# A hybrid attention and recurrence block on one core: the rank of a pair's operations, and which projections stand beside the first and the last pair

## The chip, the cores and the metric

The kernel runs on one core of a Trainium2 chip. The metric is device time in microseconds (us) of one execution, the median of several runs. A core has TensorE (PE; its weight loads are PEld), VectorE (DVE), ScalarE (ACT), GpSimd (POOL) and SyncE (SP). Each works through its own queue in order. DMA transfers are issued here by SP and POOL.

## The reference

One transformer-like block on 256 tokens of width 2048, with a context of 256 tokens that serves attention and the start state of the recurrence. All in float32:

```python
mod = silu(c) @ w_ada + b_ada;  shift, scale, gate = split(mod, 3)
xn = rmsnorm(x) * (1 + scale) + shift        # the same for the context: cn
aq, ak, av, ag, hq, hff, hfb, hi, hg, ma, mb = split(xn @ w_in)    # w_in: 2048 x 19456
att = window_attention(rope(aq), rope(ak), av, k_ctx, v_ctx, sink) * silu(ag)
f = lb + (1 - lb) * sigmoid(z)               # z: hff forward, hfb backward; 16 heads of 128
s_f, s_b = final states of the context's recurrences
o = forward scan + backward scan of S <- f * S + (1 - f) v^T, read with silu(hq)
hg_branch = rmsnorm(o, per head) * silu(hg)
y = sigmoid(ma + b0) * (hg_branch @ w_o_hgrn) + sigmoid(mb + b1) * (att @ w_o_attn)
out = rmsnorm(x + gate * (y @ w_out))
```

## The kernel before, in words

**A projection in chunks.** TensorE multiplies float32 as high and low parts in the type fp32r. A chunk of weights is 512 KB: SP loads it into one of four `raw` buffers (L66), ScalarE copies the high part into `wh` (L76), VectorE subtracts to get the low part `wl` (L77), three buffers each, and TensorE runs matmuls high by high, low by high and high by low (L91, L92 and L94 where tokens are stationary, L145 and L148 where weights are). The generators `proj_tok_g` (8 chunks) and `proj_col_x_g` (4 chunks) yield after each chunk, so that chunks can be placed between other work. Their sums lie in two of four PSUM banks `pj`.

**Order.** A scheduler orders each engine's instructions ahead of time, by a simulated time line: among those that could run it takes the one that ranks highest. Rank is program order, raised by `tc.high_priority(...)`; a chunk's two splits are raised by `PRIO` (L75), a pair's operations are not raised. In blocks with `manual_schedule` TensorE keeps the program's order; instructions outside of such a block can be placed into its gaps.

**Stages.** First norms, modulation and the first forget gates. Then the input stage (to about 655 us): values, keys and forget gates, with `quad_tok` and `quad_col` (a Strassen-like form of the product, seven products per block, L592 to L670). Each of the 13 calls of `quad_col` writes forget gates `F` (a tile of tag `F0`, two buffers) to DRAM, and then takes a step of `gate` (L670): the last third of the modulation, the vector `gate` of the reference, is computed on VectorE, 32 chunks of `w_ada` at two instructions each (L201 to L203). In the input stage its weights go through POOL's queue into an `F0` buffer too (`wg`, L193), later through SP's into `raw`.

**Pairs.** Then the 16 heads of the recurrence in eight pairs, from L1157. `load_forgets` brings the gates of both directions back (tags `F0`, and `F1` with one buffer) and `ctx_decay` scans the context's part on VectorE (L776 to L781). `pair` is a generator of small operations: the context's decays are turned on TensorE (L921), products grow over levels 1 to 64 on VectorE (`grow`, L899 to L905) with copies on ScalarE (`copies`, L831 and L834), blocks of decay-weighted scores come from matmuls of 32 rows (`level`, L858), then the state at the middle (`own`, L979, and L984 on VectorE), the output (`ob`, L996 to L998), the norm (L1004, L181, L182, L1008) and, as `turned`, the transposition into `bH` and `bL` (L1016 to L1022), which the output projection reads; `turned` runs early in the next pair.

A pair yields how many steps of TensorE work shall follow (1.5, 0.5, 1.5, 3, 1 and 1, together 8.5 steps of two chunks), and `weave` puts chunks of other projections there: `inputs` takes 13 items of `side_work` (output gates, merge gates, attention gates; nine items each, of which eight are chunks) and the next pair's query projection (4 chunks). For the last pair it takes 17 items and what is left of the side work. `with_gates` adds a step of `gate` after every six chunks. The first query projection (L1162) stands directly ahead of the first pair.

**After the pairs.** `part_a` (L1180) multiplies the recurrence's branch by `w_o_hgrn` in four blocks of 512 columns, eight chunks each; the chunk at row 256 k needs heads 2 k and 2 k + 1. A step of `gate` is taken ahead of every second chunk. Then attention, the second output projection and the final one with its norm.

Of the kernel before, what the change touches and what calls it, by code (L numbers as in the profile page):

```python
# [14 lines left out]
P = 128  # L15
# [6 lines left out]
PRIO = 100000  # L22
# [16 lines left out]
def block_kernel(ctx: ExitStack, tc: tile.TileContext, x, c, cx, c_ctx, w_ada, b_ada, norm_gain, w_in,  # L39
# [29 lines left out]
    def wchunk(w, row0, nk, col0, ncol):  # L69
        cl = col0 if isinstance(col0, tuple) else (col0,)  # L70
        raw, rv = wload(w, row0, nk, cl, ncol)
        h = wp.tile([P, 1024], F32R, tag="wh", name="wh", bufs=3)
        lo = wp.tile([P, 1024], F32R, tag="wl", name="wl", bufs=3)
        n = len(cl) * nk * ncol
        with tc.high_priority(PRIO):  # L75
            act.activation(h[:, :n], raw[:, :n], AF.Copy)  # L76
            dve.tensor_tensor(lo[:, :n], raw[:, :n], h[:, :n].bitcast(F32), op=ALU.subtract)  # L77
        parts = [(h[:, g * nk * ncol: (g + 1) * nk * ncol].rearrange("p (k c) -> p k c", k=nk),
                  lo[:, g * nk * ncol: (g + 1) * nk * ncol].rearrange("p (k c) -> p k c", k=nk)) for g in range(len(cl))]
        return parts if isinstance(col0, tuple) else parts[0]  # L80
# [6 lines left out]
    def mm_high_first(parts):  # L87


        for o, s, m, first, _ in parts:  # L90
            pe.matmul(o, s[0], m[0], start=first, stop=False)  # L91
            pe.matmul(o, s[1], m[0], start=False, stop=False)  # L92
        for o, s, m, _, last in parts:
            pe.matmul(o, s[0], m[1], start=False, stop=last)  # L94

    def bank(name="pj"):
        return pj.tile([P, 512], F32, tag="pj", name=name)

    def proj_tok_g(w, col0, src, toks):


        banks = [bank() for _ in toks]
        for k0 in range(0, KT, 2):
            h, lo = wchunk(w, k0 * P, 2, col0, 512)
            mm_high_first([(banks[i], src(k0 + j, t), (h[:, j, :], lo[:, j, :]), k0 + j == 0, k0 + j == KT - 1)
                           for j in range(2) for i, t in enumerate(toks)])
            yield len(toks) * 6 * 512
        return banks
# [126 lines left out]
    with pl("st", reuse_waits="tile") as st:  # L235
# [201 lines left out]
        def take(g, n):  # L437
            for _ in range(n):
                next(g, None)
# [71 lines left out]
    def pairs_of(a):  # L511
        return a.rearrange("p (a t) -> p a t", a=2)

    def run(g):
        for _ in g:
            pass
# [26 lines left out]
    gate = gates()  # L543

    with pl("sp", reuse_waits="tile") as sp:
# [74 lines left out]
        def quad_col(d, h0):  # L620

            co = (C_FF, C_FB)[d] + h0 * HD
            b = {n: wload(w_in, 1024 * (n[0] == "2"), 8, (co + HD * (n[1] == "2"),), HD)[0]
                 for n in ("11", "12", "22", "21")}
            m_ = [bank8() for _ in range(3)]
            into = {0: (0, True), 1: (1, True), 2: (0, False), 3: (1, False), 4: (0, False), 5: (2, True), 6: (0, False)}
            sg = [base.tile([P, 512], F32, tag="sm", name="sg", bufs=3) for _ in range(2)]
            s15 = fp.tile([P, 2, 512], F32, tag="F1", name="s15")
            su = None

            def joined(m, s, dst):


                dve.tensor_tensor(s, m, s, op=ALU.add)
                dve.tensor_tensor(dst, pairs_of(s[:, :T]), pairs_of(s[:, T:]), op=ALU.add)

            for (i, _, mv), src in zip(ORDER, combos(b)):
                h, lo = [a.rearrange("p (k c) -> p k c", k=8) for a in two(src)]
                z, fresh = into[i]
                for k in range(8):  # L640
                    pe.matmul(m_[z].rearrange("p (z a t) -> p z a t", z=2, a=2), h[:, k, :], mv(k),  # L641
                              start=fresh and k == 0, stop=False, skip_group_check=True)
                for k in range(8):
                    pe.matmul(pairs_of(m_[z][:, :T]), lo[:, k, :], mv(k)[:, 0], start=False, stop=k == 7,  # L644
                              skip_group_check=True)
                with tc.high_priority(2 * PRIO):
                    if i < 2:
                        act.activation(s15[:, i, :], m_[i], AF.Copy)
                    elif i == 2:
                        su = base.tile([P, 512], F32, tag="bb", name="su", bufs=2)  # L650
                        act.activation(su, m_[0], AF.Copy)
                    elif i == 3:
                        joined(m_[1], su, half(sg[1], 0))
                    elif i == 4:
                        u3 = base.tile([P, 512], F32, tag="bb", name="u3", bufs=2)
                        act.activation(u3, m_[0], AF.Copy)
                        joined(u3, s15[:, 1, :], half(sg[1], 1))
                    elif i == 5:
                        joined(m_[2], s15[:, 0, :], half(sg[0], 0))
                    else:  # L660
                        act.activation(half(sg[0], 1), pairs_of(m_[0][:, T:]), AF.Copy)
                        dve.tensor_tensor(half(sg[0], 1), pairs_of(m_[0][:, :T]), half(sg[0], 1), op=ALU.add)
            F = fp.tile([P, 2, 512], F32, tag="F0", name="F0", bufs=2)
            for i in (1, 0):
                act.activation(sg[i], sg[i], AF.Sigmoid)
                act.activation(F[:, i, :], sg[i], AF.Identity, scale=lbc[:, 2 + d, h0 + i: h0 + i + 1],
                               bias=lbc[:, d, h0 + i: h0 + i + 1])
            nc.gpsimd.dma_start(F_dr[d][h0 // 2], F.rearrange("p i t -> p (i t)"))
            wg_at[:] = ["F0", 2]
            take(gate, 1)  # L670

        def quad_tok(col0, dst):

# [87 lines left out]
    bH = hp.tile([P, KT, T], F32R, name="bH")  # L761
    bL = hp.tile([P, KT, T], F32R, name="bL")
# [267 lines left out]
    def weave(g, filler):  # L1030

        ahead = 0
        for want in g:
            ahead -= want * STEP
            while ahead < 0:
                got = next(filler, None)
                if got is None:
                    break
                ahead += got
        run(filler)  # L1040
# [53 lines left out]
    def attn_gates(j):  # L1094
        for hf in range(2):
            bg = yield from proj_col_x_g(w_in, C_G + 512 * j + 256 * hf)
            for i, b in enumerate(bg):
# [4 lines left out]
                c0 = (2 * hf + i) * T  # L1102
                nc.gpsimd.dma_start(cg_dr[j][:, c0: c0 + T], sg)

    def load_forgets(n):
        F = [fp.tile([P, 2, 512], F32, tag=f"F{d}", name=f"F{d}", bufs=2 - d) for d in range(2)]
        for d in (1, 0):
            nc.gpsimd.dma_start(F[d].rearrange("p i t -> p (i t)"), F_dr[d][n])
        ctx_decay(F)
        return F  # L1110
# [5 lines left out]
            yield 0  # L1116

    side = side_work()
    SIDE = (13, 13, 13, 13, 13, 13, 13, 17)

    def inputs(n, res):

        units, F = 0, None
        for _ in range(SIDE[n]):
            got = next(side, None)
            if got is None:
                break
            units += got
            if F is None and n < 7 and units >= 4 * STEP:
                F = load_forgets(n + 1)  # L1130
            yield got
        if n < 7:
            F = F or load_forgets(n + 1)
            res[:] = [F, (yield from proj_col_x_g(w_in, C_HQ + 2 * (n + 1) * HD))]
        else:
            run(side)

    def with_gates(filler):

# [17 lines left out]
    with tc.manual_schedule(engines={mybir.EngineType.PE}):  # L1157
        wg_at[:] = []
        count = [0]
        grps = [[None] * 3 for _ in range(4)]  # L1160
        res = [load_forgets(0), None]
        res[1] = result(proj_col_x_g(w_in, C_HQ))  # L1162
        for n in range(8):
            if n % 2 == 0:
                load_values(n // 2, grps[n // 2])
                load_gate(n // 2, grps[n // 2])
            nxt = [None] * 2
            weave(pair(n // 2, n % 2, grps[n // 2], *res), with_gates(inputs(n, nxt)))
            res = nxt
            if n == 0:  # L1170
                attn_values()
        for f in done:
            f()

    def b_st(kt, t):
        sl = slice(t * P, (t + 1) * P)
        return bH[:, kt, sl], bL[:, kt, sl]


    def part_a(n):  # L1180
        by = proj_tok_g(w_oh, n * 512, b_st, range(2))
        for z in range(4):
            take(gate, 1)
            for _ in range(2):
                next(by)
        by = result(by)
        for t in range(2):
            dve.tensor_tensor(y[n][:, t, :], by[t], y[n][:, t, :], op=ALU.mult)
# [5 lines left out]
    for n in range(4):  # L1194
        part_a(n)
# [337 lines left out]
```

## Time and profile before

| | us |
|---|---|
| median of 3 runs | 1642.47 |
| lowest, highest run | 1642.16, 1650.26 |
| profiled execution, its own time | 1636.88 |
| its span, first to last instruction | 1635.1 |
| TensorE busy | 1578.3 |
| VectorE, ScalarE busy | 1190.2, 870.4 |
| mean granted TensorE clock | 0.992 |

The profile is of one execution. A row of a group gives line, engine, operation, tiles written and read, shapes, count, then busy time in us and the mean of one in ns, then the idle time of the engine ahead of them and what ended it. A row of the timeline gives start, duration, engine, line, tiles, shapes and count, and in brackets the idle time ahead and its releaser. The granted clock is a share of full speed. Tile names are those of the program, without buffer numbers.

### The profile page before, as it was taken

How to read it: one execution, taken by the hardware profiler on the slowest of the kernel's cores; microseconds unless marked ns; L12 is line 12 of the kernel's file. 1: busy time of each engine (PE TensorE's matmuls, PEld its weight loads, DVE VectorE, ACT ScalarE, POOL GpSimd, SP SyncE). 2: the span in 40 equal slices, each digit the busy share in tenths (PEclk: the TensorE clock that was granted, in tenths of full speed). 3: DMA queues.
4: the chain of work that ended last, by engine and by line, in shares of the span. 5: the costliest groups of instructions: out<-in, count | busy, mean ns of one | idle time of the engine just before them, and what ended most of it. 6: DMA issues, size and time to landing. Idle time of an engine off the chain costs nothing.

```text
span 1635.1 us, 27367 instructions
## 1 busy us (share of the span) xinstructions
PE 1578.3 (97%) x10810; PEld 1345.8 (82%) x10810; DVE 1190.2 (73%) x1745; ACT 870.4 (53%) x1356; POOL 105.8 (6%) x216
## 2 busy tenths in 40 slices
PE   7999999999999999799999999999999999899998
PEld 4667899999888888678878878788888878788887
DVE  4449677777888888678787878876656778656764
ACT  4334433434566666466665666666344666754442
POOL 2000000000000000111101110111000000000000
PEclk9999999999999999899999999999999999999999
DMA  9994533344455554766667667666665543367662
GB/s 370 386 365 155 167 130 129 131 132 136 132 174 169 165 163 156 255 225 200 229 213 248 207 204 239 207 213 229 201 190 181 160 129 103 118 235 233 219 196 88
DMA packets 234177, 318.06 MB, mean 195 GB/s; under 512 B 10400, under 2 KB 154176, under 8 KB 233280
## 3 DMA queue, kind: packets, MB, share of 16 engines
q1 hardware_dynamic: 217360, 260.03, 48.9%
q0 software_dynamic: 15968, 55.17, 9.6%
q8 instruction: 85, 1.39, 0.3%
q10 hardware_dynamic: 720, 1.11, 0.2%
q14 instruction: 44, 0.36, 0.1%
HBM read 292.67 MB, written 23.60 MB: 193 GB/s over the span
## 4 chain that ended last, share of the span: by engine, by line
PE 78%; DVE 8%; DMA 6%; ACT 4%; issue 4%; POOL 0%; DVEq 0%; POOLq 0%; ACTq 0%
PE pj L91 11%; PE pj L92 11%; PE pj L94 11%; PE pj L145 5%; PE pm L641 4%; PE pj L641 4%; PE pj L722 2%; PE pj L719 2%; PE pj L717 2%; PE pm L644 2%; PE pj L644 2%; DVE wl L77 2%; PE pj L148 2%; PE pa L319 2%; PE pm L722 2%
## 5 line engine op out<-in xcount | busy, mean ns | idle before, releaser
L77 DVE TENSOR_TENSOR wl<-raw,wh 128x1024 fp32r<-128x1024 f32 x292 | 354.7, 1221 | 170.9 <-ACT wh L76 165.8
L76 ACT ACTIVATE wh<-raw 128x1024 fp32r<-128x1024 f32 x292 | 307.3, 1060 | 275.8 <-PE pj L92 194.5
L91 PE MATMUL pj<-wh,xHL 128*128 128x512 f32 (+1 forms) x704 | 275.9, 394 | 1.2 <-ACT sg L218 0.7
L92 PE MATMUL pj<-wh,xHL 128*128 128x512 f32 (+1 forms) x704 | 270.3, 386 | 0.0
L94 PE MATMUL pj<-wl,xHL 128*128 128x512 f32 (+1 forms) x704 | 183.4, 385 | 0.4 <-DVE wl L77 0.4
L91 PEld LDWEIGHTS pj<-wh,xHL 128*128 128x128 f32 x704 | 132.8, 189 | 28.1 <-ACT sg L218 1.9
L92 PEld LDWEIGHTS pj<-wh,xHL 128*128 128x128 f32 x704 | 132.8, 189 | 24.6
L94 PEld LDWEIGHTS pj<-wl,xHL 128*128 128x128 f32 x704 | 130.1, 188 | 27.3 <-DVE wl L77 0.8
L616 ACT ACTIVATE wh<-raw 128x1024 fp32r<-128x1024 f32 x92 | 97.3, 1058 | 91.1 <-PE pj L719 28.2
L145 PE MATMUL pj<-xHL,wh 128*128 128x512 f32 x512 | 135.0, 406 | 1.6 <-ACT F L831 1.6
L616 ACT ACTIVATE wh<-T 128x1024 fp32r<-128x1024 f32 x69 | 73.2, 1060 | 110.0 <-DVE T L597 40.0
L617 DVE TENSOR_TENSOR wl<-raw,wh 128x1024 fp32r<-128x1024 f32 x92 | 111.8, 1220 | 21.9 <-ACT wh L616 21.7
L145 PEld LDWEIGHTS pj<-xHL,wh 128*128 128x128 f32 x512 | 94.9, 194 | 20.0 <-ACT F L831 1.8
L617 DVE TENSOR_TENSOR wl<-T,wh 128x1024 fp32r<-128x1024 f32 x69 | 84.2, 1221 | 24.6 <-ACT wh L616 24.1
L92 PE MATMUL pj<-wh,bL 128*128 128x512 f32 x256 | 99.5, 391 | 0.0
L91 PE MATMUL pj<-wh,bH 128*128 128x512 f32 x256 | 99.4, 390 | 0.0
L148 PEld LDWEIGHTS pj<-xHL,wl 128*128 128x128 f32 x512 | 70.4, 191 | 5.4
L148 PE MATMUL pj<-xHL,wl 128*128 128x256 f32 x512 | 71.6, 283 | 0.0
L94 PE MATMUL pj<-wl,bH 128*128 128x512 f32 x256 | 70.1, 391 | 0.0
L904 DVE TENSOR_TENSOR A<-A,X 128x512 f32<-128x512 f32 x96 | 61.9, 686 | 2.4 <-ACT Kmt L834 1.3
L597 DVE TENSOR_TENSOR T<-raw,T 128x1024 f32<-128x1024 f32 x46 | 56.2, 1221 | 0.5
L91 PEld LDWEIGHTS pj<-wh,bH 128*128 128x128 f32 x256 | 48.1, 188 | 10.0
(368 smaller groups left out, 3055.5 us busy)
## 6 DMA issues: line engine op xcount, KB each, us to landing
raw<-in_w_in_dram SPq DMA_DIRECT2D x300, 512.0 KB, 3.9
raw<-in_w_ada_dram SPq DMA_DIRECT2D x83, 512.0 KB, 7.7
raw<-in_w_o_hgrn_dram SPq DMA_DIRECT2D x32, 512.0 KB, 4.0
raw<-in_w_o_attn_dram SPq DMA_DIRECT2D x32, 512.0 KB, 4.2
F<-F POOLq DMA_DIRECT2D x29, 512.0 KB, 4.6
raw<-in_w_out_dram SPq DMA_DIRECT2D x28, 512.0 KB, 3.6
wg<-in_w_ada_dram POOLq DMA_DIRECT2D x13, 512.0 KB, 6.2
v<-vo POOLq DMA_DIRECT2D x8, 512.0 KB, 3.1
```

The costliest lines, as they stand in the source:

```text
L76: act.activation(h[:, :n], raw[:, :n], AF.Copy)
L77: dve.tensor_tensor(lo[:, :n], raw[:, :n], h[:, :n].bitcast(F32), op=ALU.subtract)
L91: pe.matmul(o, s[0], m[0], start=first, stop=False)
L92: pe.matmul(o, s[1], m[0], start=False, stop=False)
L94: pe.matmul(o, s[0], m[1], start=False, stop=last)
L145: pe.matmul(o.rearrange("p (a t) -> p a t", a=2), h[:, j, cs_], xHL[:, :, k0 + j, :T], start=k0 + j == 0, stop=False)
L148: pe.matmul(o[:, :T], lo[:, j, cs_], xH[:, k0 + j, :T], start=False, stop=k0 + j == KT - 1)
L616: act.activation(h, src, AF.Copy)
L617: dve.tensor_tensor(lo, src, h.bitcast(F32), op=ALU.subtract)
L641: pe.matmul(m_[z].rearrange("p (z a t) -> p z a t", z=2, a=2), h[:, k, :], mv(k), start=fresh and k == 0, stop=False, skip_group_check=True)
L644: pe.matmul(pairs_of(m_[z][:, :T]), lo[:, k, :], mv(k)[:, 0], start=False, stop=k == 7, skip_group_check=True)
L722: pe.matmul(o, st_(4 * s + k)[:, 0, z, :], lo[:, k, :], start=False, stop=s == 1 and k == 3 and z == 1, skip_group_check=True)
```

## The change

Four things change:

1. In `weave` each step of `pair` is made under `high_priority(2 * PRIO)`, and so is the first `load_forgets`: a pair's operations rank above the chunks' splits.
2. The first output gate (9 items of side work, 8 chunks) is computed ahead of the first query projection.
3. The last pair takes the remaining 8 items of the side work and then 7 of the 8 chunks of the first block of `part_a`, whose eighth chunk stays behind the pair.
4. The last four calls of `quad_col` (h0 of 12 and 14) take no step of `gate`.

```diff
@@ quad_col
-            take(gate, 1)
+            if h0 < 12:
+                take(gate, 1)
@@ weave
-        for want in g:
+        while True:
+            with tc.high_priority(2 * PRIO):
+                want = next(g, None)
+            if want is None:
+                break
             ahead -= want * STEP
@@
+    first_a = proj_tok_g(w_oh, 0, b_st, range(2))
@@
-    SIDE = (13, 13, 13, 13, 13, 13, 13, 17)
+    SIDE = (13, 13, 13, 13, 13, 13, 13, 8)
@@ inputs, the last pair
-            run(side)
+            yield from side
+            for _ in range(7):
+                yield next(first_a)
@@ ahead of the pairs
-        res = [load_forgets(0), None]
+        with tc.high_priority(2 * PRIO):
+            res = [load_forgets(0), None]
+        take(side, 9)
         res[1] = result(proj_col_x_g(w_in, C_HQ))
@@ part_a
-        by = proj_tok_g(w_oh, n * 512, b_st, range(2))
-        for z in range(4):
+        by = first_a if n == 0 else proj_tok_g(w_oh, n * 512, b_st, range(2))
+        for z in range(1 if n == 0 else 4):
             take(gate, 1)
-            for _ in range(2):
-                next(by)
+            take(by, 1 if n == 0 else 2)
```

`take(g, n)` advances a generator n times; `b_st`, which hands out `bH` and `bL`, is only moved up.

More of the change, by code (lines that the diff above doesn't have):

```diff
@@ L1103, in attn_gates, with b_st @@
                 nc.gpsimd.dma_start(cg_dr[j][:, c0: c0 + T], sg)
+    def b_st(kt, t):
+        sl = slice(t * P, (t + 1) * P)
+        return bH[:, kt, sl], bL[:, kt, sl]
+    first_a = proj_tok_g(w_oh, 0, b_st, range(2))
     def load_forgets(n):
@@ L1173, in block_kernel @@
             f()
-    def b_st(kt, t):
-        sl = slice(t * P, (t + 1) * P)
-        return bH[:, kt, sl], bL[:, kt, sl]
     def part_a(n):
-        by = proj_tok_g(w_oh, n * 512, b_st, range(2))
-        for z in range(4):
+        by = first_a if n == 0 else proj_tok_g(w_oh, n * 512, b_st, range(2))
+        for z in range(1 if n == 0 else 4):
             take(gate, 1)
-            for _ in range(2):
-                next(by)
+            take(by, 1 if n == 0 else 2)
         by = result(by)
```

## The prediction

> **What bounds the kernel now.** I read the page first, then the busy time by stage, then what TensorE waited for.
>
> ```profile
> PE 1578.3 (97%) x10810; PEld 1345.8 (82%) x10810; DVE 1190.2 (73%) x1745; ACT 870.4 (53%) x1356; POOL 105.8 (6%) x216
> ```
> ```profile
> 140.00:655.00 515.00, 514.16 (x3390) 472.76 (x3389) 419.24 (x443) 258.16 (x308) 26.37 (x46) 1.00 0.47 148
> 655.00:692.00 37.00, 26.71 (x135) 22.95 (x134) 25.20 (x36) 18.09 (x27) 4.67 (x16) 0.86 0.70 255
> 692.00:1128.00 436.00, 417.52 (x4156) 356.81 (x4155) 346.40 (x584) 275.16 (x527) 50.31 (x106) 0.99 0.67 219
> 1128.00:1235.00 107.00, 107.00 (x496) 88.85 (x495) 60.76 (x73) 44.82 (x56) 5.07 (x9) 1.00 0.64 201
> ```
>
> The columns are the stretch, its length, busy PE, PEld, DVE, ACT and POOL, the granted clock, the DMA share and GB/s. TensorE is the bound, and its work does not change, so the change can only win back idle time and slow clock. The input stage (140 to 655) and the first output projection (1128 to 1235) have none to give. The seam at 655 to 692 lacks 10.3 us, the pairs (692 to 1128) lack 18.5 us. The waits of TensorE name them, the seam's first (whole run), then the pair stage's:
>
> ```profile
> PE tw L921 <- DVE F L781: 10.3, 1, 10.3
> ```
> ```profile
> PE ob L998 <- DVE X L984: 10.5, 6, 3.0
> PE al L858 <- ACT so L834: 3.6, 2, 1.8
> PE pj L145 <- ACT F L831: 1.6, 1, 1.6
> PE kt L964 <- DVE A L904: 1.5, 7, 0.4
> ```
>
> Idle time also costs clock afterwards. Short stretches behind three stalls:
>
> ```profile
> 679.40:683.00 3.60, 3.60 (x13) 3.23 (x14) 3.47 (x7) 1.92 (x4) 0.00 (x0) 0.53 0.13 27
> 848.30:852.00 3.70, 3.70 (x31) 3.61 (x32) 2.04 (x5) 1.22 (x9) 0.00 (x0) 1.00 0.46 161
> 951.60:956.00 4.40, 4.14 (x43) 3.22 (x44) 4.23 (x8) 2.44 (x5) 0.00 (x0) 0.61 0.78 256
> 1057.60:1062.00 4.40, 4.35 (x14) 3.37 (x15) 4.40 (x7) 2.53 (x4) 1.08 (x2) 0.61 0.69 204
> ```
>
> Behind the 10.3 us stall the clock stands at 0.53 for 3.6 us, a loss of 3.6 x 0.47 = 1.7 us. Behind two of the short stalls it is 0.61 for 4.4 us: 2 x 4.4 x 0.39 = 3.4 us. So the seam costs 10.3 + 1.7 = 12.0 us, the pairs 18.5 + 3.4 = 21.9 us, and 33.9 us is the most that the change can win.
>
> [...]
>
> **The seam: an output gate ahead of the first pair, and no gate chunk in the last four column products.** What pair 0 waited for stands in the timeline (start, duration, engine, line, idle before):
>
> ```profile
> 643.88 0.56 POOL L668 DMA_DIRECT2D F<-F  x1 [14.62 <-ACT F L666]
> 656.36 0.71 POOL L194 DMA_DIRECT2D wg<-in_w_ada_dram  x1
> 657.65 0.55 POOL L1108 DMA_DIRECT2D F<-F  x1 [0.38 <-DVE sg L635]
> 669.83 0.53 POOL L1108 DMA_DIRECT2D F<-F  x1 [6.21 <-DVE acc L203]
> ```
> ```profile
> 667.99 1.54 DVE L203 SCALAR_TENSOR_TENSOR acc<-wg,cg,acc 128x512 f32<-128x512 f32 x2 [3.00 <-DMA wg<-in_w_ada_dram]
> 668.00 1.11 PE L148 MATMUL pj<-xHL,wl 128*128 128x256 f32 x8
> 678.61 0.68 DVE L781 SCALAR_TENSOR_TENSOR F<-F,e 128x512 f32<-128x512 f32 x1
> 679.40 1.94 PE L921 MATMUL tw<-cs,F 128*128 128x128 f32 x8 [10.29 <-DVE F L781]
> ```
>
> The last gate chunk (wg) takes one of the two F0 buffers at 656.36, lands at 668 and is used up at 669.5. Only then may pair 0's forward forgets load into that buffer, and their scans and L781 end at 679.3. TensorE ran dry at 669.1.
>
> ```profile
> F<-F POOLq DMA_DIRECT2D x29, 512.0 KB, 4.6
> ```
>
> Two edits meet here. Without the gate chunk, the F0 buffer whose content was stored at 643.88 is free at about 648.5 (4.6 us for such a store), so that load moves forward by some 15 us or more; F1 still loads at 657.65, behind L635. And eight chunks of the output gate now stand between the column products and the query projection. One chunk is 2.73 us of TensorE, by the start of the same group in two successive chunks:
>
> ```profile
> 1130.43 1.08 PE L94 MATMUL pj<-wl,bH 128*128 128x512 f32 x4
> 1133.16 1.07 PE L94 MATMUL pj<-wl,bH 128*128 128x512 f32 x4
> ```
>
> Eight are 21.8 us: TensorE has work to 669.1 + 21.8 = 690.9, and needs L781 then, not at 669. Even if nothing came earlier, 679.3 would be 11.6 us in time. So the 12.0 us goes, and the clock behind it.
>
> What is late next is weights. The loads of raw issued between 652 and 672, and the two splits that free a buffer:
>
> ```profile
> DMA to landing us min/median/max: 6.4/9.3/10.2
> ```
> ```profile
> L77 DVE TENSOR_TENSOR wl<-raw,wh 128x1024 fp32r<-128x1024 f32 x292 | 354.7, 1221 | 170.9 <-ACT wh L76 165.8
> L76 ACT ACTIVATE wh<-raw 128x1024 fp32r<-128x1024 f32 x292 | 307.3, 1060 | 275.8 <-PE pj L92 194.5
> ```
>
> With four buffers a chunk can come every (9.3 + 1.06 + 1.22) / 4 = 2.9 us, at 10.2 us every 3.1, against 2.73: over eight chunks 1.4 to 3 us, and nothing where the gate chunk that is gone makes the loads quicker. Bounds 0 and 3 us; I take 1, since the buffers start full. The gain is 11 us, with 9 and 12 as ends.
>
> **The gate chunks moved.** The pair loop has 20 gate steps before (124 half-step chunks, one in six) and 20 after (123). Four leave the column products, so three chunks and the closing sum end up in the first output projection, with three loads on SP's queue instead of POOL's.
>
> ```profile
> L203 DVE SCALAR_TENSOR_TENSOR acc<-raw,cg,acc 128x512 f32<-128x512 f32 x34 | 25.5, 749 | 25.4 <-DMA raw<-in_w_ada_dram 25.2
> L904 DVE TENSOR_TENSOR A<-A,X 128x512 f32<-128x512 f32 x96 | 61.9, 686 | 2.4 <-ACT Kmt L834 1.3 <-ACT F L831 0.5
> L905 DVE TENSOR_TENSOR X<-X 128x256 f32<-128x256 f32 (+5 forms) x48 | 11.7, 243 | 1.3
> ```
>
> Three chunks are 6 x 0.749 = 4.5 us of VectorE in a stage where it is busy 60.8 of 107 us and TensorE all of it: nothing. If one of these loads were late, the ring of raw buffers behind it would stop for a chunk, 2.7 us; that is the cost without cover.
>
> **Pairs above chunks.** One wait in its order (third pair):
>
> ```profile
> 843.72 1.06 PE L979 MATMUL al<-v,Kmt 128*128 128x128 f32 x8
> 844.39 2.36 DVE L77 TENSOR_TENSOR wl<-raw,wh 128x1024 fp32r<-128x1024 f32 x2 [3.85 <-ACT wh L76]
> 846.67 0.75 DVE L156 TENSOR_TENSOR hsum<-pj,hsum 128x256 f32<-128x256 f32 x2
> 847.34 1.11 DVE L984 SCALAR_TENSOR_TENSOR X<-so,X,al 128x128 f32<-128x128 f32 x4
> 848.25 0.49 PE L998 MATMUL ob<-X,A 128*128 128x128 f32 x2 [3.02 <-DVE X L984]
> ```
>
> L984 could start when the own state is there (844.8), but two weight splits and a sum of the next pair's queries stand ahead of it. With the pair on top it comes first, save for a split already running (up to 1.2 us). A pair asks for 8.5 steps, 17 chunks, and gets 16 or 15. Where it has 16, a chunk of 2.7 us lies between the own state and L998, and the wait goes. Where it has 15 (pairs 2, 4 and 6), three L984 of the four must pass while TensorE has 0.45 us of L996 and L997: 0.85 - 0.45 = 0.4, with part of a split about 1.0 each. So 10.5 becomes 3.
>
> The al, pj and kt waits (3.6 + 1.6 + 1.5, and small ones to 18.5 in all) come out of the chain of L904 and copies under 6 chunks (16.4 us) of cover; each of its nine links can meet a split. Not being queued behind two of them, but still behind one that runs, I take half: 8.0 becomes 4. The clock loss 3.4 becomes 1, as fewer stalls cause it. Together 21.9 becomes 8: 14 us.
>
> On the other side the splits are served later. In those 6 chunks VectorE owes the pair 12 x 0.686 + 6 x 0.243 = 9.7 us and the chunks 6 x 1.221 = 7.3: 17.0 in 16.4 us and the matmuls of the levels. The lag is under a microsecond by this, and two finished chunks (5.5 us) cover it. What it costs without the cover is the fourth rival's price. Bounds 0 and 14 us (all given back); I take 4, nearer the lag that the rows give. Net 10 us.
>
> **The last pair.** It had 15 chunks and gets 7 + 7 = 14; the output projection's first seven need only heads 0 to 13. Before, this work was taken there anyway: the matmuls on bH at 1130 and 1133 above lie ahead of the pair's own end, in
>
> ```profile
> 1136.76 0.39 PE L998 MATMUL ob<-so,A 128*128 128x128 f32 x2
> ...
> 1140.61 1.12 DVE L1008 SCALAR_TENSOR_TENSOR so<-ob,ss,gate 128x128 f32<-128x128 f32 x4
> ...
> 1146.26 0.48 ACT L1021 ACTIVATE bH<-to,cols 128x256 fp32r<-128x256 f32 x1 [1.43 <-PE to L1016]
> ```
>
> and TensorE was idle nowhere from 1128 on. So this edit has nothing to win, and it uses up the cover: from the last L998 to the end of L1008 are 4.6 us, and transposes, L1021 and its rest add about 1.7 (0.44 + 2 x 0.48 and the hand-over): 6.3 us before heads 14 and 15 are there. The eighth chunk waits for them and holds one of three wh buffers, so only two chunks of the next block, 5.5 us, can be pulled ahead. That leaves 0.8; the own state with one chunk of cover less, and L984 right before L998, add some 1.7. I take a loss of 2.5 us, between 0 and 6.3.
>
> **Sum.** -11 - 10 + 2.5 = -18.5 us on the profiled execution of 1636.9 us (span 1635.1): 1618.4. The median of the three runs, 1642.47, is 5.6 us above that execution, and I apply the difference to it: 1624.
>
> **Rivals.** First, the order on VectorE gives back all that it wins (pair waits go, splits come late by as much): only seam and tail count, 1642.5 - 11 + 2.5 = 1634. For it: VectorE is busy 346 of 436 us, and 17.0 of 16.4 us in the long step. Against: the waits named are mostly one short instruction behind two long ones.
>
> Second, the seam only changes its wait: loads of eight more chunks don't keep up in a stretch of 255 GB/s, and half of the 12 us returns as waits for raw: 1624 + 5 = 1629. Against: among the waits of TensorE in the pair stage, at 219 GB/s, stands no load.
>
> Third, all goes: 33.9 us, less nothing at the tail: 1609.
>
> Fourth, slower. The order is fixed ahead, and VectorE takes its instructions in that order; a pair's L904 put ahead of a split waits there for its copies on ScalarE, and the split behind it waits too.
>
> ```profile
> L834 ACT ACTIVATE Kmt<-A 128x512 f32<-128x512 f32 x30 | 20.7, 715 | 15.1 <-DVE A L904 14.5 <-DVE A L899 0.6
> ```
>
> A round has two copies, 1.43 us; four rounds are 5.7 us of VectorE standing still in the long step, against one finished chunk of 2.7: 3.0 us a pair, 24 us over eight, none of the old waits gone: 1642.5 - 11 + 2.5 + 24 = 1658. It decides from 16.7 / 8 = 2.1 us a pair on. For it: L203 already stood 25.2 us at VectorE's head, waiting for its load. Against: L904 itself stood for copies only 1.8 us in 96. [...]
>
> **How the numbers follow.** My forecast 0.50 (1617 to 1631); first rival 0.17, second 0.12, third 0.12, fourth 0.09. Half a per cent, 8.2 us, is about what a measurement of this kernel can tell from no change: faster means below 1634.3. The first rival lies on that line and gives half to "same"; with a little of the second: faster 0.80, same 0.11, slower 0.09. The range to leave out two in ten takes in most of the first three rivals: 1612 to 1638.
>
> **What would show it.** Right: no wait at tw L921 in the seam, and clock 1.00 there; L984 directly behind L979 on VectorE, ob waits near 3 us; the last gate chunks behind 1128 instead of ahead of it; TensorE short of about 2 us of work after the last pair. Wrong: waits of L91, L94, L145 or L148 for wh or wl in the pair stage above 10 us in sum, waits for raw above 4 us in the seam, or a stall above 6 us ahead of the eighth chunk of the output projection.

## The result and the profile after

Twenty executions of each kernel in turn gave a median of 1638.63 us (1634.11 to 1643.91) for the changed kernel and 1643.97 us (1637.27 to 1650.26) for the one before: a ratio of 0.9967, 95% interval 0.9955 to 0.9979, or 5.3 us won where 18.5 were forecast. That is within the half per cent that the prediction calls no change. The profiled execution of the changed kernel, with a span of 1642.1 us, was the slowest of its twenty, and the one of the kernel before, with 1635.1, was faster than any of its twenty; so medians say how much, and the profiles say where.

The page of the changed kernel, and its busy time in the stages for which the prediction showed the rows of before (same columns: stretch, length, PE, PEld, DVE, ACT, POOL, granted clock, DMA share, GB/s), with a last stretch just behind the pairs:

```profile
PE 1583.3 (96%) x10810; PEld 1349.7 (82%) x10810; DVE 1187.6 (72%) x1745; ACT 871.6 (53%) x1356; POOL 99.4 (6%) x212
```
```profile
655.00:692.00 37.00, 37.00 (x188) 31.55 (x187) 24.40 (x29) 19.56 (x23) 6.08 (x17) 1.00 0.90 313
692.00:1128.00 436.00, 410.62 (x3985) 352.16 (x3984) 340.91 (x583) 268.55 (x514) 46.11 (x104) 0.98 0.64 213
1128.00:1180.00 52.00, 48.45 (x345) 38.96 (x345) 34.72 (x54) 25.68 (x47) 5.07 (x9) 0.97 0.69 224
```

In the seam TensorE is now busy all of 37 us at full clock: the 10.3 us are gone. But the pairs lack 436 - 410.6 = 25.4 us instead of 18.5, and the first output projection, where TensorE had never been idle, lacks 3.6. What was won at 655 to 692 has come back behind it as idle time. What TensorE waited for in the changed kernel from 690 to 1180 us (total us, times, longest):

```profile
PE ob L999 <- DVE X L985: 10.3, 6, 3.5
PE pj L145 <- DVE hsum L156: 6.7, 1, 6.7
PE kt L965 <- DVE A L905: 3.9, 6, 3.0
PE pj L92 <- DVE bL L1023: 2.2, 2, 1.8
PE al L980 <- ACT X L871: 2.1, 1, 2.1
PE pj L91 <- DVE sgm L1069: 1.0, 1, 1.0
PE al L980 <- ACT Kmt L968: 0.9, 1, 0.9
```

From L672 on the line numbers are one higher than before, and from `weave` on five or more: L985 is the old L984, L999 the old L998. The wait of `ob` for the state in the middle, which the prediction cut from 10.5 to 3 us, stands at 10.3. And a wait that the prediction does not know, 6.7 us of a query projection (L145) for a sum that drains a PSUM bank (L156), is the second largest. In a second profile of the same kernel (the run `again` below) it reads 5.4:

```profile
PE ob L999 <- DVE X L985: 9.6, 6, 2.3
PE pj L145 <- DVE hsum L156: 5.4, 1, 5.4
```

The idle time of the pair stage can be added up from the rows: 5.1 us more at the bank (6.7, and 1.6 before at the same place), 3.5 in the last pair and behind it, from 1128 on (2.2 + 0.9 + 0.4), 2.4 at `kt`, 2.1 at `al`, 1.7 where the third pair starts (L91), less 0.2 at `ob`, 2.8 at the old `al` wait and 1.3 of small ones: 10.5, which is 25.4 + 3.6 - 18.5.

Two things were to be found out: why the rank, which was to bring 10 us net, leaves the largest wait as it was, and where the bank's wait comes from. My theory after the result: the rank does nothing where L985 stands, since the planner's time line has L985 ready only behind the splits; and the bank's wait comes from the shift of the side work, not from the rank. The rival is the prediction's first one: the rank wins at some places and gives it back at others, the bank among them.

### The profile page after: what moved, and what is told of

It reads as the page before. It is cut to its first block, busy times and chain, and to the rows that moved or that the text cites. A ratio compares the mean times of both kernels' runs of the same rounds, so it can differ in the third digit from the quotient of the medians.

```text
span 1642.1 us, 27394 instructions
## 1 busy us (share of the span) xinstructions
PE 1583.3 (96%) x10810; PEld 1349.7 (82%) x10810; DVE 1187.6 (72%) x1745; ACT 871.6 (53%) x1356; POOL 99.4 (6%) x212
## 4 chain that ended last, share of the span: by engine, by line
PE 71%; DVE 11%; DMA 8%; issue 5%; ACT 4%; SPq 0%; POOL 0%; DVEq 0%; POOLq 0%; ACTq 0%
PE pj L91 11%; PE pj L92 11%; PE pj L94 10%; PE pj L145 5%; DMA raw<-in_w_in_dram 4%; DMA raw<-in_w_ada_dram 3%; PE pj L148 2%; PE pj L723 2%; PE pj L720 2%; PE pj L718 2%; DVE wl L617 2%; DVE wl L77 2%; PE pm L641 2%; PE pj L641 2%; PE pm L723 2%
## 5 line engine op out<-in xcount | busy, mean ns | idle before, releaser
L76 ACT ACTIVATE wh<-raw 128x1024 fp32r<-128x1024 f32 x292 | 307.4, 1059 | 273.4 <-PE pj L92 187.7
L91 PE MATMUL pj<-wh,xHL 128*128 128x512 f32 (+1 forms) x704 | 275.2, 393 | 2.4 <-DVE sgm L1069 1.0
L92 PE MATMUL pj<-wh,xHL 128*128 128x512 f32 (+1 forms) x704 | 270.0, 385 | 0.0
L94 PE MATMUL pj<-wl,xHL 128*128 128x512 f32 (+1 forms) x704 | 183.3, 385 | 0.0
L91 PEld LDWEIGHTS pj<-wh,xHL 128*128 128x128 f32 x704 | 132.5, 188 | 29.6 <-ACT sg L218 1.9
L92 PEld LDWEIGHTS pj<-wh,xHL 128*128 128x128 f32 x704 | 132.5, 188 | 24.6
L94 PEld LDWEIGHTS pj<-wl,xHL 128*128 128x128 f32 x704 | 130.2, 188 | 26.5
L145 PE MATMUL pj<-xHL,wh 128*128 128x512 f32 x512 | 135.5, 408 | 6.7 <-DVE hsum L156 6.7
L145 PEld LDWEIGHTS pj<-xHL,wh 128*128 128x128 f32 x512 | 95.7, 196 | 25.0 <-DVE hsum L156 6.9
L92 PE MATMUL pj<-wh,bL 128*128 128x512 f32 x256 | 99.8, 393 | 2.2 <-DVE bL L1023 2.2
L91 PE MATMUL pj<-wh,bH 128*128 128x512 f32 x256 | 100.2, 396 | 0.4 <-ACT wh L76 0.4
L94 PE MATMUL pj<-wl,bH 128*128 128x512 f32 x256 | 70.2, 391 | 0.0
L92 PEld LDWEIGHTS pj<-wh,bL 128*128 128x128 f32 x256 | 48.1, 189 | 12.9 <-DVE bL L1023 3.3
L91 PEld LDWEIGHTS pj<-wh,bH 128*128 128x128 f32 x256 | 48.5, 189 | 10.9 <-ACT wh L76 0.7
```

The lines of the kernel that those rows point to most:

```text
L145: pe.matmul(o.rearrange("p (a t) -> p a t", a=2), h[:, j, cs_], xHL[:, :, k0 + j, :T], start=k0 + j == 0, stop=False)
```

## The experiments

Every ratio is against the kernel before, run in turn on the same chip. Diffs are against the changed kernel where nothing else is said. The first seven ask which part of the change does what.

**again**: the changed kernel once more, beside the others.

> The changed kernel once more, for a second profile beside that of the execution of 1642.1 us span. Rank theory (the pair's rank leaves L985 behind the splits and lets the draining of PSUM banks come late, which costs): the wait of an L145 or L91 for a drained bank comes back, 3 to 9 us in sum in the pair stage, and the waits ob <- X stay near 10 us. Noise theory (the 6.7 us at 1076 were one late load): no wait for a drained bank above 1.5 us, span about 1635. Time against before by both: 0.9967 (0.9955 to 0.9979), some 5 us less.

0.9947 [0.9926, 0.9968], 1636.61 us. It overlaps the first comparison; what follows is held against both. The bank's wait is back with 5.4 us, so it was no single late load.

**rank_off**: the change without its rank.

```diff
-        while True:
-            with tc.high_priority(2 * PRIO):
-                want = next(g, None)
-            if want is None:
-                break
+        for want in g:
```

> The changed kernel, but weave makes a pair's steps at their own rank, as before; the seam and the last pair as changed. Rank theory: the rank costs about 8 us (6.7 + 1.0 + 0.7 of waits for drained banks in the profile, and slow clock behind them), so this is 6 to 10 us faster than the changed kernel, ratio to before about 0.992. Rival, rank of no weight (it only swaps neighbours): within 2 us of the changed kernel, 0.997. My prediction, rank gains 10 us: 10 us slower than the changed kernel, 1.003.

0.9964 [0.9948, 0.998], 1640.08 us; `ob` 9.5 us, the bank 4.4. So the bank's wait does not come from the rank.

**rank_only**: the kernel before, with the rank in `weave` alone (the reverse of the diff above).

> The kernel before with only the pairs raised in weave. Rank theory: 4 to 9 us slower than before, 1.0025 to 1.0055, with waits of L91 or L145 for a drained bank. Rank of no weight: 1.000 within 0.001. My prediction: 10 us faster, 0.994.

0.9976 [0.996, 0.9991], 1642.42 us. Its waits in the pair stage, and its timeline at the third pair, the place that the prediction showed (its L984 is the old number):

```profile
PE ob L998 <- DVE X L984: 11.8, 6, 3.5
PE al L858 <- ACT so L834: 3.9, 2, 2.2
PE pj L145 <- DVE sgm L1068: 1.2, 1, 1.2
```
```profile
845.55 1.06 PE L979 MATMUL al<-v,Kmt 128*128 128x128 f32 x8
846.72 2.36 DVE L77 TENSOR_TENSOR wl<-raw,wh 128x1024 fp32r<-128x1024 f32 x2 [3.85 <-ACT wh L76]
848.99 0.75 DVE L156 TENSOR_TENSOR hsum<-pj,hsum 128x256 f32<-128x256 f32 x2
849.66 1.11 DVE L984 SCALAR_TENSOR_TENSOR X<-so,X,al 128x128 f32<-128x128 f32 x4
850.57 0.79 PE L998 MATMUL ob<-X,A 128*128 128x128 f32 x2 [3.51 <-DVE X L984]
```

The same two splits and the same sum stand ahead of L984 as before, although L984 now ranks above both. It is so in all eight pairs: held against each other instruction by instruction, by line and tiles, the traces of the two kernels have the same four VectorE instructions just ahead of L984 in every pair, two splits among them, and the changed kernel and rank_off agree there in the same way. The rank does act elsewhere: here up to 13 of VectorE's 1745 instructions stand in another place, between rank_off and the changed kernel up to 48, between two executions of one kernel none. Note the 3.85 us that VectorE stands idle ahead of the splits: its next instruction, the split, waits for ScalarE's copy (L76), and when the own state (L979) ends, at 846.6, the split becomes ready at nearly the same moment. There is no wait of L94 for `wl` beyond 0.8 us either: the splits are not served later, so the rank has neither the gain nor the price that the prediction gave it.

**seam_only**: the kernel before with the seam's edits alone, the raised first `load_forgets` among them (no rank in `weave`, no output projection in the last pair, which keeps eight side items).

```diff
-            take(gate, 1)
+            if h0 < 12:
+                take(gate, 1)
...
-    SIDE = (13, 13, 13, 13, 13, 13, 13, 17)
+    SIDE = (13, 13, 13, 13, 13, 13, 13, 8)
...
+        take(side, 9)
```

> The kernel before with only the seam changed: no gate step in the last four column products, the first load of forgets raised, the first output gate ahead of the first query projection, the last pair left with 8 items of side work; no raised pairs, and the first block of the output projection wholly behind the pairs. Rank theory with the prediction's seam: -11 to -12 us, 0.993. Rival, the seam gives only about 5 us and the other parts nothing: 0.997, like the changed kernel. TensorE's wait at tw L921 gone by both.

0.9951 [0.9933, 0.997], 1638.44 us: 8.1 us by the ratio, as much as the whole change. Its waits from 690 to 1180 us:

```profile
PE ob L999 <- DVE X L985: 10.6, 7, 3.7
PE pj L145 <- DVE hsum L156: 4.0, 1, 4.0
PE kt L965 <- DVE A L905: 3.9, 7, 2.6
PE pj L94 <- DVE wl L77: 3.0, 2, 2.7
PE al L859 <- ACT qk L835: 1.9, 1, 1.9
```

The bank's wait is here without rank and without the last pair's edit: the seam's edit makes it. There is also a new wait of 1.9 us in the last pair (`al` for `qk`), which now has less to cover it.

**ahead_only**: seam_only, but the column products keep their gate chunks, so that only the eight chunks in front are new.

```diff
-            if h0 < 12:
-                take(gate, 1)
+            take(gate, 1)
```

> The seam without its first edit: an output gate ahead of the first pair as in seam_only, but the last four column products take their gate steps as before, so that the forward forgets wait again for a buffer held by wg. Prediction's reading (the eight chunks alone are cover enough, 11.6 us to spare): no wait at tw L921, and within 2 us of seam_only (0.995). Rival (both are needed): a wait at tw L921 of 3 us or more.

0.9945 [0.9926, 0.9964], 1638.25 us, no wait at `tw`, TensorE busy all of 655 to 692. The eight chunks are enough by themselves, as the prediction worked out ("even if nothing came earlier, 679.3 would be 11.6 us in time"); the gate edit beside them wins nothing.

**before_again**: a second profile of the kernel before.

> The kernel before once more, for a second profile; its first profiled execution (1636.9 us) was among the fastest of its 31 timed ones (1640 to 1652 in the last comparison). Theory that the profile I predicted from showed too little waiting: more idle time or slow clock in the pair stage (above the 28.7 us between the first tw and the last ob), span 1640 to 1648. Rival, the pair stage is the same and the difference lies outside of the span or in the first stage: idle 28 to 30 us there, span about 1635.

1640.96 us, span 1639.2, `tw` 10.8 us, 18.3 us idle from 692 to 1128. The stalls that the prediction started from are the same in a slower execution of that kernel.

**bank_fix**: the changed kernel with one side chunk taken from the seventh pair and given to the last one. By the seam's nine items the seventh pair's last side chunk had become the first of the second attention gate, where it had been the first of the first. It takes the two banks that were free, and leaves the query projection behind it those of a block that ended only a chunk before; with one chunk less the block ends with the pair, and the free banks are the query projection's.

```diff
-    SIDE = (13, 13, 13, 13, 13, 13, 13, 8)
+    SIDE = (13, 13, 13, 13, 13, 13, 12, 9)
```

> The changed kernel with 12 items of side work beside the seventh pair and 9 beside the last, instead of 13 and 8: the seventh pair then ends with the whole of the first attention gate, and no chunk of the second stands between that gate's last bank and the query projection, which needs a bank. Bank theory (the shift of the side work by one output gate made TensorE wait 4.0 to 6.7 us for a bank not yet drained, hsum L156, ahead of L145, in all three kernels with the seam edit, and slow clock behind it): that wait falls below 1 us; 4 to 8 us faster than the changed kernel. Rival (the drain is late whatever stands there, since VectorE and ScalarE are behind in that step): the wait moves to another matmul with 3 us or more, time within 2 us of the changed kernel.

0.9932 [0.9907, 0.9957], 1634.47 us, and its waits no longer hold the bank:

```profile
PE ob L999 <- DVE X L985: 9.9, 6, 2.7
PE kt L965 <- DVE A L905: 4.7, 7, 2.3
PE al L980 <- ACT X L871: 1.2, 1, 1.2
```

That is 2.5 to 5.8 us beside the two comparisons of the changed kernel. How the wait comes about stands in the timeline of the changed kernel:

```profile
1069.04 1.11 PE L148 MATMUL pj<-xHL,wl 128*128 128x256 f32 x8
...
1072.48 0.64 ACT L155 ACTIVATE hsum<-pj 128x256 f32<-128x256 f32 x2
1072.67 0.75 DVE L203 SCALAR_TENSOR_TENSOR acc<-raw,cg,acc 128x512 f32<-128x512 f32 x1 [1.10 <-DMA raw<-in_w_ada_dram]
1073.34 1.29 DVE L905 TENSOR_TENSOR A<-A,X 128x512 f32<-128x512 f32 x2
1074.55 0.75 DVE L203 SCALAR_TENSOR_TENSOR acc<-raw,cg,acc 128x512 f32<-128x512 f32 x1
1075.21 1.22 DVE L77 TENSOR_TENSOR wl<-raw,wh 128x1024 fp32r<-128x1024 f32 x1
1076.35 0.75 DVE L156 TENSOR_TENSOR hsum<-pj,hsum 128x256 f32<-128x256 f32 x2
1076.82 0.79 PE L145 MATMUL pj<-xHL,wh 128*128 128x512 f32 x1 [6.67 <-DVE hsum L156]
```

The matmuls at 1069 are the end of that chunk, and the query projection (1076.82) needs a bank that the sum L156 still has to read. L156 has the lowest rank there and stands behind a gate chunk that waits for its load (L203), a growth step, the second half of the gate chunk and a split. TensorE stands 6.7 us. VectorE's order is only half of that: ScalarE's copy L155, which the sum needs, is done at 1073.12, 3.0 us after the chunk's end at 1070.15, and the sum then stands another 3.2 us behind the others. Nor does the place alone make the wait. In the kernel before, too, the seventh pair ended one chunk into a block, but the bank was a merge gate's, which one VectorE sum empties without a copy. The sum came within a microsecond of that chunk's end at 1056.0, and TensorE waited 1.6 us at 1057.62 (the profile puts that wait down to L831):

```profile
1056.78 1.29 DVE L1064 TENSOR_TENSOR sgm<-pj,bb 128x512 f32<-128x512 f32 x2
```

The next four ask what the waits of `ob` are worth and whether they can be had.

**shift_step**: the step of 3.0 ahead of the own state cut to 2.5, so that L985 comes half a step earlier against the splits.

```diff
-        yield 3.0
+        yield 2.5
```

> The changed kernel with yield 2.5 instead of 3.0 after the first level matmuls, so that the pair asks for 16 chunks and one or two of them come to lie between own (L980) and ob (L999). Theory that the ob wait comes from L985 standing behind the splits of the chunks that follow, by the order and not by rank, and can only be covered by work: ob waits fall from about 9.6 us to below 4, while al and kt waits (0.4 to 3.0 now) grow by one chunk's cover at most, 2.7 us a pair where the chain is late: between 6 us faster and 6 slower than the changed kernel, my guess 2 us faster. Rival, VectorE puts two splits ahead of L985 again wherever it stands: ob waits stay near 10 us.

0.994 [0.992, 0.9961], 1635.69 us. From 692 to 1180 TensorE is idle 24.4 us, 26.4 in the second profile of the changed kernel. Its waits:

```profile
PE al L859 <- ACT so L835: 8.7, 5, 3.5
PE kt L965 <- DVE A L905: 8.0, 9, 3.9
PE pj L145 <- DVE hsum L156: 5.6, 1, 5.6
```

No wait of `ob` is left, and `al` and `kt` have taken its place: with less cover ahead of them the levels come late. A wait moved is not a wait won.

**no_state_wait**: bank_fix, but `ob` reads the start state instead of the state in the middle, so that nothing waits for L985. It leaves the state in the middle out of the output.

```diff
-                pe.matmul(o, A[:, 2, ht], (S2 if t else S)[:, 0, i, :], start=False, stop=False)
-                pe.matmul(o, A[:, 1, ht], (S if t else S2)[:, 1, i, :], start=False, stop=True)
+                pe.matmul(o, A[:, 2, ht], S[:, 0, i, :], start=False, stop=False)
+                pe.matmul(o, A[:, 1, ht], S[:, 1, i, :], start=False, stop=True)
```

> bank_fix, but the output matmuls (ob, L999) read the start state S where they should read the state at the middle, S2; L985 still runs, nobody waits for it (the output is not the reference's). It takes the ob waits away without making them short. Theory A (these waits were winnable: the 10.5 us that I had named): bank_fix's 10 us of ob waits go and nothing replaces them, 8 to 12 us faster than bank_fix (0.9932), ratio about 0.987. Theory B (the pair's chain is longer than its cover, so a wait taken away in one place comes up at the next link, as in shift_step): al, kt and own waits grow by most of it, less than 4 us faster than bank_fix.

0.9854 [0.9828, 0.988], 1621.66 us (1620.24 to 1622.68): 12.8 us less than bank_fix by the ratios. So the state's wait was worth winning, and no single wait takes its place. In the two profiles the idle time from 692 to 1180 us differs by only 4.5 us, though 9.9 us of `ob` are gone: the other waits are some 5.5 us longer in sum, none of them by more than 1.3 (bank_fix's profile is of its fastest execution). The rest of the 12.8 is seen in the medians alone.

**best_side** and **fold**: first another division of the side work over the pairs, then the state in the middle taken out of the way. The output of a half is q (tot S + K v): its second part can be had as (q K) v, scores first. So four score matmuls take the place of the four transpositions of K, `ob` gets a fourth matmul, and the own state (L980) with its four L985 goes; what is left for VectorE is tot S, which is ready early.

```diff
-    SIDE = (13, 13, 13, 13, 13, 13, 12, 9)
+    SIDE = (13, 14, 12, 13, 14, 12, 12, 9)
```
```diff
-                pe.transpose(kt[...], A[:, 3 * d, ...], ident)
+                pe.matmul(kt[...], A[:, 3 * d, ...], A[:, 2 - d, i * T + (1 - d) * P: i * T + (2 - d) * P], start=True, stop=True)
...
-        yield 1.0
-        (own: 4 matmuls of KT and v; S2 = S * tot + own, 4 scalar_tensor_tensor)
-        yield 1.0
+        (S2 = S * tot, 4 tensor_scalar)
+        yield 2.0
...
+                pe.matmul(o, KT[:, c0: c0 + HD], v[:, 1 - t, hv], start=False, stop=True)
```

> bank_fix with the side work dealt out as 13, 14, 12, 13, 14, 12, 12, 9 items, so that each pair's query projection starts either behind a whole gate or three and more chunks into one. Bank theory: the 0.9 and 0.7 us at the start of the third pair (L91 for sgm and hsum) go as well, and nothing else changes: 1 to 3 us faster than bank_fix. Rival (pairs with fewer chunks lose cover): the ob waits of the pairs that lost a chunk grow by 1 to 2 us each, no gain.

> best_side, and the state at the middle is no longer made: where q read S2 = tot S + K v, the output matmuls read tot S (computed ahead, on VectorE) and the product of the scores q K (four matmuls of 128 x 128 in place of the four transpositions, copied to SBUF by ScalarE as before) with v. The same result by another order of the sums, 0.3 us more matmul a pair, and no VectorE instruction between two matmul groups at the end of a pair. Theory A (the wait for L985 was winnable, 12.8 us in no_state_wait against bank_fix): no wait of ob for VectorE, 6 to 11 us faster than best_side, ratio 0.986 to 0.989. Theory B (the order puts splits ahead of whatever comes last, so ob waits for the copy of the scores instead): ob waits of 8 us or more behind ScalarE, within 3 us of best_side (0.9924).

best_side: 0.9924 [0.9903, 0.9945], 1633.11 us, not to be told from bank_fix. fold: 0.9874 [0.9854, 0.9895], 1624.68 us (1620.97 to 1626.56): 8 us less than best_side by the ratios, some 21 less than the kernel before, with the whole computation in it. Its stages and its largest waits (in its own line numbers):

```profile
692.00:1128.00 436.00, 423.68 (x4193) 363.90 (x4192) 351.64 (x602) 277.55 (x530) 49.70 (x107) 0.99 0.68 220
1128.00:1235.00 107.00, 105.51 (x499) 87.52 (x498) 63.64 (x80) 45.97 (x62) 4.51 (x8) 1.00 0.67 211
```
```profile
PE kt L965 <- DVE A L905: 6.7, 5, 3.0
PE to L1008 <- DVE so L1000: 2.5, 2, 2.3
PE pj L94 <- DVE wl L77: 2.3, 2, 1.3
PE ob L986 <- ACT X L881: 1.4, 2, 1.2
```

The pairs lack 12.3 us instead of 25.4, and `ob` waits for no state any more. This is the version that beats both kernels.

The last four ask for the rank and the last pair's edit once more, without the bank's wait that lay over them.

**fix_norank** and **fold_norank**: bank_fix and fold with the diff of rank_off.

> bank_fix with the pairs at their own rank. Second estimate of the rank's worth, in a kernel without the wait for a bank. From rank_only (3.7 us) and again against rank_off (3.5 us): 2 to 5 us slower than bank_fix, 0.995 to 0.996. Rival, rank of no weight: within 1.5 us. ob waits near 10 us by both.

> fold with the pairs at their own rank: the rank's worth where the wait that it could not reach is gone. From the three earlier comparisons (3.7, 3.5 and 0.5 us): 0 to 4 us slower than fold. Rank of no weight: within 1 us. Rank harmful: faster by more than 1 us.

0.9937 [0.9916, 0.9958], beside 0.9932 with the rank; 0.9875 [0.9856, 0.9895], 1623.96 us, beside 0.9874. Without the bank's wait no worth of the rank can be seen.

**fix_nolast** and **fold_nolast**: bank_fix and fold without the chunks of the output projection in the last pair, which then has nine side items and no more.

```diff
             yield from side
-            for _ in range(7):
-                yield next(first_a)
```

> bank_fix without the last pair's share of the output projection: the last pair has 9 items of side work and then whatever the planner pulls ahead. Prediction's reading (this edit can win nothing, and loses 2.5 us behind the last pair): not slower than bank_fix, 0 to 3 us faster; TensorE idle less than 1 us behind the last pair. Rival (planned chunks beside the last pair are worth something): 1 us or more slower.

> fold without the last pair's share of the output projection. The prediction's reading (nothing to win): within 1 us of fold or faster. What fix_nolast against bank_fix says (3.7 us): 2 to 5 us slower than fold, with idle TensorE in the last pair.

By the timed runs 0.9962 [0.9949, 0.9976] beside 0.9932, and 0.9907 [0.9884, 0.9929] beside 0.9874: about 5 us lost each time, though the intervals overlap in both. The waits of fold_nolast from 690 to 1180 us, and two stretches of it:

```profile
PE kt L965 <- DVE A L905: 6.7, 4, 3.5
PE al L859 <- ACT qk L835: 4.6, 1, 4.6
```
```profile
1100.00:1120.00 20.00, 15.42 (x259) 13.03 (x258) 14.52 (x27) 8.62 (x17) 1.64 (x3) 0.92 0.72 227
1120.00:1140.00 20.00, 20.00 (x146) 16.29 (x145) 14.14 (x23) 12.64 (x24) 1.62 (x3) 0.90 0.73 241
```

With only nine side items beside it, too little covers the levels of the last pair: 4.6 us of standing still, and 20 us at a clock of 0.90 behind it, 2 us more.

## Why the prediction was right or wrong

**The seam: right, but for its small term.** No wait at `tw`, clock 1.00, as told. The 1 us taken off for late loads of `raw` was 0: the loads kept up at 313 GB/s and TensorE waited for none, where the stretch had carried 255 before. The step that was too careful took landing times of 9.3 to 10.2 us, met in the old seam, as a bound for the new one. With that the second rival falls, and in its own stretch the seam's gain is the whole 12 us.

**Pairs above chunks: wrong.** The step that failed is "With the pair on top it comes first, save for a split already running (up to 1.2 us)". It took the order on VectorE as a choice between instructions that are all ready, and read from the trace that L984 could start at 844.8, when the own state was there. But the splits stand ahead of L984 in the traces with the rank just as without it, in all eight pairs: `ob` waits 11.8 us with the rank alone, 10.3 and 9.6 in the change, 10.5 before, where 3 was told. That the rank doesn't move L984 is shown by these orders. Why is argued: the order is fixed ahead by simulated times, rank only decides between what is ready in that simulation, and the splits and the own state become ready within some 0.1 us of each other in the trace of rank_only. That the simulated time line has the splits ready first is not shown, as that time line stands in no trace. The other two terms of that part, 4 us won at the small waits and 2.4 us of clock, didn't come either (the small waits grew, and the granted clock in the pairs was 0.98 in both profiles of the change, 0.99 in both of before), and the 4 us given back by late splits were 0: L94 waits for no `wl` in the changed kernel's rows. So the 10 us net came to something between 0 and 4, by four pairs of kernels: 3.9 us for the rank alone, 2.8 between again and rank_off (-0.5 if the first comparison stands for the changed kernel), 0.8 between bank_fix and fix_norank, 0.2 between fold and fold_norank. The first interval just clears one, and the two of each other pair overlap. How much of it is real stays open. The first rival named the size nearly rightly (a rank worth nothing on balance), but not the reason: the pair waits did not go, so nothing of them could be given back.

**What was left out.** The part on the seam priced the place that work is moved to, and not the place that it is moved from. Eight chunks in front shift all side work behind them by nine items, and which block ends just ahead of a query projection decides which PSUM bank it waits for and what has to empty it. A wait of 3.8 to 6.7 us follows in all five kernels that have this shift (ahead_only and seam_only among them, which lack the other parts); rank_only, without it, waits 1.2 there, and bank_fix not at all. Behind the stall the clock is gone too, in the changed kernel here:

```profile
1076.80:1081.00 4.20, 4.18 (x11) 3.46 (x12) 4.20 (x8) 2.23 (x6) 0.94 (x2) 0.50 0.75 247
```

4.2 x 0.5 is 2.1 us more. None of the prediction's marks pointed there: the one for weights in the pair stage speaks of waits for `wh` and `wl`, and this wait is for a drain.

**The last pair: the idle time about right, the edit's worth wrong.** A loss of 2.5 us was told and TensorE short of some 2 us behind the pair; it lacks 3.6 and 3.9 in the two profiles, of which 2.2 in the first are the wait for heads 14 and 15 (L92 for L1023) that was meant, less in bank_fix (1.1, by the stretch below), and between rank_off and seam_only, which differ in this edit alone, lie about 2 us the same way, within their intervals.

```profile
1128.00:1180.00 52.00, 50.92 (x262) 42.01 (x252) 33.52 (x48) 23.56 (x40) 5.06 (x9) 1.00 0.75 239
```

But "this edit has nothing to win, and it uses up the cover" held it against a last pair with 17 items, which the seam's edit has just halved. Against the pair that it really replaces, it wins about 5 us where the bank's wait is out of the way, twice, though each time within overlapping intervals. In the changed kernel itself this gain doesn't show; that the bank's wait hid it is likely, but no run shows it.

**The gate chunks moved, and the fourth rival.** No cost of the three moved chunks shows, as told. The fourth rival (a growth step ahead of a split, 24 us) did not come: with so few of VectorE's instructions in another place, there was little that could bring it. The third's 33.9 us were not reached by any version: fold, with fold_norank the fastest that computes the whole, wins some 21, and it does so by taking the state away and not by an order.

**The sum.** It is made from before_again and again, whose executions lie nearer to their medians than the first two. The rows of before_again, then those of again, for the seam, the pairs and what lies behind:

```profile
655.00:692.00 37.00, 26.17 (x131) 22.52 (x130) 24.85 (x37) 17.69 (x26) 5.77 (x18) 0.82 0.71 253
692.00:1128.00 436.00, 417.73 (x4140) 356.79 (x4140) 346.63 (x584) 272.48 (x520) 50.10 (x106) 0.99 0.67 217
```
```profile
692.00:1128.00 436.00, 413.48 (x4006) 353.74 (x4005) 345.70 (x592) 273.59 (x520) 47.79 (x106) 0.98 0.67 216
1128.00:1180.00 52.00, 48.12 (x349) 38.80 (x348) 35.59 (x52) 23.18 (x40) 4.54 (x8) 1.00 0.70 223
```

Idle time: -10.8 in the seam, +4.2 in the pairs (22.5 for 18.3), +3.9 behind them, where there was none; busy time of TensorE over the whole span, for 10810 matmuls in both, 1580.4 to 1578.3, -2.1, which I put down to the clock. Together -4.8, with -6.0 between the two spans and -5.3 between the medians. The prediction had -11 with its clock, -10 and +2.5: the seam holds, the term behind the pairs is some 1.4 us short, and the pairs, told 10 us shorter, stand 4.2 longer. There it was wrong, by a rank that doesn't move the instruction it was meant for and by a bank that it did not see.

## What to carry to other kernels

A rank is no promise of an order: compare the orders with and without it at the wait that it is meant for, and look whether the engine was idle just before. Where the order stays, as here, change what must be waited for (here the state). Work moved forward leaves a hole where it stood and renumbers what stands behind it: go through the new neighbours of each stage boundary, buffers and PSUM banks too, before the sum is made. And a wait that goes at one place is only won if the sum of idle time falls; in shift_step the whole of the largest wait went, and hardly any time with it.

## What the runs showed of the hardware

Two executions of the same changed kernel, with nearly the same waits, differ by 8.9 us in span (1642.1 and 1633.2), and 5.0 of that is busy time of TensorE for the same 10810 matmuls. The second profile's page and its stretch behind the bank's wait:

```profile
PE 1578.3 (97%) x10810; PEld 1345.7 (82%) x10810; DVE 1187.1 (73%) x1745; ACT 871.5 (53%) x1356; POOL 100.1 (6%) x212
```
```profile
1072.48:1076.68 4.20, 4.20 (x14) 3.54 (x15) 4.20 (x8) 2.33 (x6) 0.96 (x2) 0.59 0.79 241
```

In the 4.2 us behind the bank's wait the granted clock was 0.59 where that wait was 5.4 us, and 0.50 where it was 6.7. The length of a stall alone does not tell the clock behind it in these traces: in the kernel before it was 0.53 behind 10.3 us and 0.61 behind waits of 1.6 and 1.8, but 1.00 behind one of 3.0. What else decides it is not shown, nor what makes up the 5.0 us between the two busy times.

Up to the first instruction in which an engine's work differs, the traces of the two kernels have the same order on that engine, with starts up to 2.2 us apart: 4109 matmuls of TensorE, 554 instructions of VectorE, 370 of ScalarE and 62 of GpSimd.

The weights' loads, at 313 GB/s and a DMA share of 0.90 in the seam, came in time for TensorE at full clock (1.00).
